# An encoder block on one Trainium2 core: the per-engine order of instructions chosen with the build tool's timeline model

## The chip, the core and the metric

The kernel runs on one NeuronCore of one Trainium2 chip. The metric is the device time of one execution in microseconds, and the time quoted is the median over runs. Engines are TensorE (PE in the profile, PEld its weight loads), VectorE (DVE), ScalarE (ACT), GpSimd (POOL) and SyncE (SP, which here only issues DMAs).

## What is computed

One encoder block over x of 512 rows and 2048 columns, all float32:

```
h   = rmsnorm(x) @ w_in                      # q, k, v, gates of both branches
a   = diff_attention(rope(q), rope(k), v)    # 8 heads, 2 softmaxes each
m   = mlstm(q', k', v', gates), both directions  # 4 heads
mix = sigmoid(branch gates) * projections of the normed a and m
x1  = x + mix @ w_out
y   = x1 + (silu(g) * u) @ w_ffn_out ;  g, u = rmsnorm(x1) @ w_ffn_in   # 5632 wide
out = rmsnorm(y)
```

In attention each head has two score matrices. Each is put through a softmax over its 512 keys, and the head uses `p = p0 - lam * p1`, then `p @ v`, then a norm over the head's 128 columns.

## The kernel before

Every float32 product is made of three products of parts: `split` (L148 to L150) copies a tile to a rounded high part on ScalarE and subtracts it on VectorE to get the low part, and `mm3` (L143 to L146) multiplies high by high, high by low and low by high. Large products use a scheme of seven block products in place of eight, so VectorE also adds weight blocks (L348 to L362) before they are split. Weights come through SP in pieces of 512 KB (`load`, L192 to L198, six raw buffers); a piece is cast to `whi_...` and subtracted to `wlo_...` (three buffers each) two pieces ahead of its use.

In time the program goes through these stages: projections for values and gates (to about 505 us), attention with the q and k projections of the next heads beside it (to 870), mLSTM (to 1000), branch projections (to 1160), the output projection wo (to 1360), the first FFN product `fi` in eleven column blocks (to 2230), and the second FFN product `fo` in two halves (to the end).

The order of the work is set in two steps. First the Python program issues instructions in an order written by hand. The projections are generators (`chunks`), and `advance(ns)` (in `build`) runs them for as many nanoseconds of TensorE work as it is given; a function handed to `later(ns, fn)` is issued when that much work has been issued since. In attention, `attn(h)` goes through four query tiles of 128 rows:

```python
        scores(0)
        advance(FILL)
        turn(0)
        scores(1)
        advance(FILL)
        turn(1)
        scores(2)
        values(0)
```

`scores(qt)` issues four products into two PSUM tiles `s{h}_{qt}_0` and `_1` (L1050, L1051), for each a maximum on VectorE (`nm`, L1052) and an exponential on ScalarE (`e`, L1054), then a reciprocal, two scalings and a sum on VectorE (L1058 to L1061). `turn(qt)` transposes that sum on TensorE into `tp{h}_{qt}` (L1071) and splits it into `pTh` and `pTl`, and `values` multiplies those by the values into `ha{h}`. `FILL` is 5600, so 5.6 us of projection products (`aqk...`, `mqk...`, `mv...`) are issued between the scores and the transposes. After the last value product of a head come a copy and a square of `ha`, its row sums on TensorE (`hss{h}`, L1108 and L1109), GpSimd's power (L544, `hrs`), and a product with a diagonal (`hbc{h}`, L551 and L552) that spreads the result over columns.

Second, the Tile framework's scheduler takes the issued instructions with their dependencies and chooses the final order on each engine by a cost model of its own; semaphores are then placed for that order. Each engine executes its list in order. Which cost model it uses is a switch of the context that `kernel` opens (L1476).

## Time and profile before

| | us |
|---|---|
| median of 3 runs | 2681.12 |
| lowest and highest | 2680.89, 2682.58 |
| profiled execution | 2683.64 |
| its span | 2681.9 |
| TensorE busy in it | 2605.4 |

The page gives busy time by engine, the span in 40 slices with the granted TensorE clock, the chain of work that ended last, and groups of instructions. An answer about waits names the engine and its operation, then what released it. A row of a timeline has a start, a duration, the engine, the line, and written tile <- read tiles; brackets hold the idle time before it.

### The profile page before, as it was taken

What the parts mean: (1) busy time and instruction counts of PE and PEld (TensorE: products, weight loads), DVE (VectorE), ACT (ScalarE), POOL (GpSimd) and SP (SyncE); (2) the same over time, 40 slices, a digit from 0 to 9 for tenths busy, and PEclk for the clock granted to TensorE, in tenths of its full rate; (3) what the DMA queues carried; (4) which work ended last, traced back from release to release, by engine and by line L of the source; (5) the groups of instructions that cost most, each with busy time, mean ns of one, the idle gap of its engine ahead of it and who ended that gap; (6) DMA issues with size and microseconds to landing.
All of it is one profiled execution on the core that took longest, in us unless ns stands there. A gap on an engine that the chain in (4) does not pass through costs nothing.

```text
span 2681.9 us, 33178 instructions
## 1 busy us (share of the span) xinstructions
PE 2605.4 (97%) x12136; PEld 2160.3 (81%) x12136; DVE 2129.2 (79%) x2692; ACT 1312.8 (49%) x1848; POOL 254.9 (10%) x448
## 2 busy tenths in 40 slices
PE   8999999999999999999899999999999999999997
PEld 7888888877878998887778888888888878777876
DVE  8977788777877676596788888888888889888885
ACT  8544444444544463345464444444444446546654
POOL 1000000011110113101110000000000002222211
PEclk9999999989999999999999999999999999999999
DMA  7655666633432346437665555555555578777763
GB/s 263 233 186 185 201 200 216 223 103 116 123 110 71 115 134 241 175 130 233 223 199 183 194 165 181 195 192 186 175 199 173 181 284 286 252 249 257 242 220 94
DMA packets 162227, 508.97 MB, mean 190 GB/s; under 512 B 21832, under 2 KB 22120, under 8 KB 162064
## 3 DMA queue, kind: packets, MB, share of 16 engines
q1 hardware_dynamic: 111456, 379.77, 41.3%
q0 software_dynamic: 33712, 97.71, 12.1%
q10 hardware_dynamic: 16896, 29.37, 3.1%
q8 instruction: 95, 1.56, 0.2%
q14 instruction: 68, 0.56, 0.1%
HBM read 445.41 MB, written 50.87 MB: 185 GB/s over the span
## 4 chain that ended last, share of the span: by engine, by line
PE 71%; DVE 12%; issue 7%; DMA 7%; ACT 2%; POOL 1%; SPq 0%; DVEq 0%; POOLq 0%; ACTq 0%
PE fi_b L145 12%; PE fi_c L145 8%; PE fi_a L145 8%; PE fo_b L145 4%; PE aqk_b L145 3%; PE fo_c L145 3%; PE fo_a L145 3%; PE mqk_b L145 3%; PE mv_p L145 3%; PE ba_p L145 3%; PE bm_p L145 3%; PE ga_b L145 2%; PE gm_b L145 2%; PE gm_a L145 1%; PE gm_c L145 1%
## 5 line engine op out<-in xcount | busy, mean ns | idle before, releaser
L145 PE MATMUL aqk_b<-xs,whi_aqk 128*128 128x512 f32 x512 | 162.0, 396 | 0.0
L149 ACT CAST whi_fi_Q<-fi_Q_t 128x1024 fp32r<-128x1024 f32 x88 | 92.5, 1052 | 117.7 <-PE fi_b L145 97.7
L145 PE MATMUL fi_a<-whi_fi_Q,h_X 128*128 128x512 f32 x440 | 147.0, 391 | 0.0
L145 PE MATMUL fi_c<-whi_fi_Q,h_S 128*128 128x512 f32 x440 | 145.0, 390 | 0.0
L145 PE MATMUL fi_b<-whi_fi_Q,h_S 128*128 128x512 f32 x352 | 115.5, 389 | 0.0
L145 PEld LDWEIGHTS aqk_b<-xs,whi_aqk 128*128 128x128 f32 x512 | 97.1, 191 | 19.6
L150 DVE TENSOR_TENSOR wlo_fi_Q<-fi_Q_t,whi_fi_Q 128x1024 fp32r<-128x1024 f32 x88 | 106.5, 1220 | 5.5 <-ACT whi_fi_Q L149 5.3
L145 PE MATMUL aqk_b<-xs,wlo_aqk 128*128 128x512 f32 x256 | 100.8, 394 | 0.0
L145 PEld LDWEIGHTS fi_c<-whi_fi_Q,h_S 128*128 128x128 f32 x440 | 83.0, 189 | 17.3
L145 PEld LDWEIGHTS fi_a<-whi_fi_Q,h_X 128*128 128x128 f32 x440 | 82.6, 188 | 16.8
L362 DVE TENSOR_TENSOR raw_fi_e<-raw_fi_e,raw_fi_f 128x1024 f32<-128x1024 f32 x44 | 53.9, 1224 | 52.6 <-DMA raw_fi_e<-in_w_ffi 52.6
L988 POOL DMA_DIRECT2D fs_X<-fg_X11d x22 | 11.9, 539 | 830.5 <-DVE wlo_fi_Q L150 785.3
L145 PE MATMUL fi_a<-wlo_fi_Q,h_X 128*128 128x512 f32 x220 | 85.9, 390 | 0.6 <-DVE wlo_fi_Q L150 0.6
L145 PE MATMUL fi_c<-wlo_fi_Q,h_S 128*128 128x512 f32 x220 | 85.8, 390 | 0.0
L348 DVE TENSOR_TENSOR raw_fi_b<-raw_fi_b,raw_fi_a 128x1024 f32<-128x1024 f32 x44 | 53.8, 1224 | 36.0 <-DMA raw_fi_b<-in_w_ffi 33.6
L149 ACT CAST whi_fi_Q<-raw_fi_e 128x1024 fp32r<-128x1024 f32 x44 | 46.4, 1055 | 72.6 <-PE fi_b L145 51.4
L145 PE MATMUL ba_p<-whi_ba,hahl 128*128 128x512 f32 x256 | 81.8, 390 | 0.0
L145 PE MATMUL mqk_b<-xs,whi_mqk 128*128 128x512 f32 x256 | 80.9, 396 | 0.0
L145 PE MATMUL bm_p<-whi_bm,hmhl 128*128 128x512 f32 x256 | 80.5, 391 | 0.0
L149 ACT CAST whi_fi_Q<-raw_fi_b 128x1024 fp32r<-128x1024 f32 x44 | 46.5, 1057 | 68.8 <-PE fi_c L145 52.1
L149 ACT CAST whi_fi_Q<-raw_fi_f 128x1024 fp32r<-128x1024 f32 x44 | 46.5, 1056 | 68.3 <-PE fi_c L145 63.9
L145 PEld LDWEIGHTS fi_b<-whi_fi_Q,h_S 128*128 128x128 f32 x352 | 66.1, 188 | 13.7
(843 smaller groups left out, 8479.5 us busy)
## 6 DMA issues: line engine op xcount, KB each, us to landing
raw_fi_a<-in_w_ffi SPq DMA_DIRECT2D x44, 512.0 KB, 3.4
raw_fi_b<-in_w_ffi SPq DMA_DIRECT2D x44, 512.0 KB, 4.2
raw_fi_c<-in_w_ffi SPq DMA_DIRECT2D x44, 512.0 KB, 4.1
raw_fi_d<-in_w_ffi SPq DMA_DIRECT2D x44, 512.0 KB, 4.2
raw_fi_f<-in_w_ffi SPq DMA_DIRECT2D x44, 512.0 KB, 3.5
raw_fi_e<-in_w_ffi SPq DMA_DIRECT2D x44, 512.0 KB, 3.6
raw_aqk<-in_w_aqk SPq DMA_DIRECT2D x32, 512.0 KB, 3.5
raw_fo_a<-in_w_ffo SPq DMA_DIRECT2D x20, 512.0 KB, 4.5
```

The source lines that it names most:

```text
L145: T.matmul(dst, lhs[l], rhs[r], start=first and i == 0, stop=last and i == 2, skip_group_check=skip)
L149: A.copy(hi, src)
L150: V.tensor_tensor(lo, src, hi.bitcast(F32), ALU.subtract)
L348: V.tensor_tensor(raws[r12], raws[r12], raws[r11], ALU.add)
L362: V.tensor_tensor(raws[r12], raws[r12], raws[r22], ALU.add)
L988: G.dma_start(got[n], fgd[g][f_].rearrange("p (k c) -> p k c", k=2))
```

## The change

The context is opened with a switch: the scheduler orders instructions by a timeline model in place of its default one. The program's own order of issue, its buffers and its arithmetic stay as they are.

```diff
-    with tile.TileContext(nc) as tc:
+    with tile.TileContext(nc, schedule_with_timeline_sim=True) as tc:
```

Of 11,527 rows that stand for TensorE's list, 9,219 lines of difference arise; VectorE's list of 2,690 rows has 3,143 and SP's of 776 has 294. Three places on TensorE follow. In the rows a product is `written<-stationary,moving` with its shape, `x2` is two such in a row, and the last number of a name is only the scheduler's.

TensorE in head 0 around the second query tile, before (`s` are scores, `tp` the transposes, `aqk2` a projection of q and k for later heads):

```order
L1051 MATMUL s0_1_0_4940<-k0_l0_4722,q0_h0_4708 128x512
L1050 MATMUL s0_1_1_4946<-k0_h1_4721,q0_h1_4709 128x512
L1051 MATMUL s0_1_1_4946<-k0_l1_4723,q0_h1_4709 128x512
L145 MATMUL aqk2_b0_4782<-xs14_4360,wlo_aqk2_30_4817 128x512
L145 MATMUL aqk2_b1_4783<-xs14_4360,whi_aqk2_30_4816 128x512 x2
L145 MATMUL aqk2_b1_4783<-xs14_4360,wlo_aqk2_30_4817 128x512
L145 MATMUL aqk2_b0_4782<-xs15_4363,whi_aqk2_30_4816 128x512 x2
L145 MATMUL aqk2_b0_4782<-xs15_4363,wlo_aqk2_30_4817 128x512
L145 MATMUL aqk2_b1_4783<-xs15_4363,whi_aqk2_30_4816 128x512 x2
L145 MATMUL aqk2_b1_4783<-xs15_4363,wlo_aqk2_30_4817 128x512
L1071 MATMUL tp0_1_4993<-ident_78,e0_1_0_4944 128x128 x4
L1050 MATMUL s0_2_0_5002<-k0_h0_4720,q0_h0_4708 128x512
```

and after:

```order
L145 MATMUL aqk2_b0_4782<-xs15_4363,wlo_aqk2_30_4817 128x512
L145 MATMUL aqk2_b1_4783<-xs15_4363,whi_aqk2_30_4816 128x512
L1051 MATMUL s0_0_1_4861<-k0_l1_4723,q0_h1_4709 128x512
L145 MATMUL aqk2_b1_4783<-xs15_4363,whi_aqk2_30_4816 128x512
L145 MATMUL aqk2_b1_4783<-xs15_4363,wlo_aqk2_30_4817 128x512
L1071 MATMUL tp0_0_4931<-ident_78,e0_0_0_4859 128x128 x4
L1050 MATMUL s0_1_0_4940<-k0_h0_4720,q0_h0_4708 128x512
L1051 MATMUL s0_1_0_4940<-k0_l0_4722,q0_h0_4708 128x512
L1050 MATMUL s0_1_1_4946<-k0_h1_4721,q0_h1_4709 128x512
L1051 MATMUL s0_1_1_4946<-k0_l1_4723,q0_h1_4709 128x512
L1071 MATMUL tp0_1_4993<-ident_78,e0_1_0_4944 128x128 x4
L1050 MATMUL s0_2_0_5002<-k0_h0_4720,q0_h0_4708 128x512
```

The ten `aqk2` products that stood between the last score product and `tp0_1` are gone from there, most of them to a place ahead of these scores; the transposes stand right behind.

TensorE in head 3 at its fourth query tile, before (rows 5 to 16 of the piece, more `aqk6` products, are left out):

```order
L1050 MATMUL s3_3_1_6185<-k3_h1_5493,q3_h1_5481 128x512
L1051 MATMUL s3_3_1_6185<-k3_l1_5495,q3_h1_5481 128x512
L145 MATMUL aqk6_b1_5976<-xs11_4281,whi_aqk6_20_5979 128x512
L145 MATMUL aqk6_b1_5976<-xs11_4281,wlo_aqk6_20_5980 128x512
...
L145 MATMUL aqk6_b0_5975<-xs15_4363,whi_aqk6_30_6047 128x512 x2
L145 MATMUL aqk6_b0_5975<-xs15_4363,wlo_aqk6_30_6048 128x512
L1071 MATMUL tp3_3_6232<-ident_78,e3_3_0_6183 128x128 x4
L1050 MATMUL s4_0_0_6276<-k4_h0_5802,q4_h0_5790 128x512
```

and after, from the third tile's transposes on:

```order
L1071 MATMUL tp3_2_6170<-ident_78,e3_2_0_6086 128x128 x4
L1050 MATMUL s3_3_0_6179<-k3_h0_5492,q3_h0_5480 128x512
L1051 MATMUL s3_3_0_6179<-k3_l0_5494,q3_h0_5480 128x512
L1050 MATMUL s3_3_1_6185<-k3_h1_5493,q3_h1_5481 128x512
L1051 MATMUL s3_3_1_6185<-k3_l1_5495,q3_h1_5481 128x512
L1071 MATMUL tp3_3_6232<-ident_78,e3_3_0_6183 128x128 x4
L1050 MATMUL s4_0_0_6276<-k4_h0_5802,q4_h0_5790 128x512
L1051 MATMUL s4_0_0_6276<-k4_l0_5804,q4_h0_5790 128x512
L1050 MATMUL s4_0_1_6282<-k4_h1_5803,q4_h1_5791 128x512
L1051 MATMUL s4_0_1_6282<-k4_l1_5805,q4_h1_5791 128x512
```

The 23 `aqk6` products that stood between `s3_3` and `tp3_3` are gone from there, and the transposes stand right behind the scores.

TensorE at the norm of head 0, beside the first tiles of head 1, before:

```order
L145 MATMUL ha0_4852<-pTl0_2_5078,av0_h1_4845 128x256
L145 MATMUL ha0_4852<-pTh0_2_5077,av0_l1_4847 128x256
L145 MATMUL aqk3_b0_5057<-xs9_4229,whi_aqk3_20_5061 128x512 x2
L145 MATMUL aqk3_b0_5057<-xs9_4229,wlo_aqk3_20_5062 128x512
L145 MATMUL aqk3_b1_5058<-xs9_4229,whi_aqk3_20_5061 128x512 x2
L145 MATMUL aqk3_b1_5058<-xs9_4229,wlo_aqk3_20_5062 128x512
...
L1108 MATMUL hss0_5257<-hsh0_5191,ones_r_85 128x512
L145 MATMUL aqk3_b0_5057<-xs12_4302,whi_aqk3_30_5119 128x512
L145 MATMUL aqk3_b0_5057<-xs12_4302,wlo_aqk3_30_5120 128x512
L1109 MATMUL hss0_5257<-hsl0_5192,ones_r_85 128x512
```

and after:

```order
L145 MATMUL ha0_4852<-pTl0_2_5078,av0_h1_4845 128x256
L145 MATMUL ha0_4852<-pTh0_2_5077,av0_l1_4847 128x256
L1108 MATMUL hss0_5257<-hsh0_5191,ones_r_85 128x512
L1109 MATMUL hss0_5257<-hsl0_5192,ones_r_85 128x512
L1071 MATMUL tp1_0_5269<-ident_78,e1_0_0_5208 128x128 x4
L1050 MATMUL s1_1_0_5278<-k1_h0_4899,q1_h0_4887 128x512
L1051 MATMUL s1_1_0_5278<-k1_l0_4901,q1_h0_4887 128x512
L1050 MATMUL s1_1_1_5284<-k1_h1_4900,q1_h1_4888 128x512
L1051 MATMUL s1_1_1_5284<-k1_l1_4902,q1_h1_4888 128x512
L552 MATMUL hbc0_5326<-hbc0_d0_5327,ones_83 128x128
```

The row sums `hss0` stand right behind the last value product `ha0`, and `hbc0` behind one tile's transposes and scores.

## Rows read from the trace of the kernel before

**Rows 1.** The page, busy time per engine, and the granted clock in 40 slices.

```profile
PE 2605.4 (97%) x12136; PEld 2160.3 (81%) x12136; DVE 2129.2 (79%) x2692; ACT 1312.8 (49%) x1848; POOL 254.9 (10%) x448
...
PEclk9999999989999999999999999999999999999999
```

**Rows 2.** The page, shares of the chain that ended last, by engine.

```profile
PE 71%; DVE 12%; issue 7%; DMA 7%; ACT 2%; POOL 1%; SPq 0%; DVEq 0%; POOLq 0%; ACTq 0%
```

**Rows 3.** Windows by stage; columns as in their first row.

```profile
core 0: us, PE busy (x) PEld busy (x) DVE busy (x) ACT busy (x) POOL busy (x), PEclk, DMA share, GB/s
...
100.00:505.00 405.00, 402.96 (x1771) 331.52 (x1771) 329.62 (x345) 197.86 (x219) 7.71 (x14) 1.00 0.62 208
505.00:870.00 365.00, 345.88 (x1748) 288.24 (x1747) 272.14 (x473) 161.05 (x290) 44.72 (x76) 0.97 0.36 109
...
1160.00:1360.00 200.00, 188.69 (x835) 152.04 (x834) 149.89 (x163) 102.25 (x156) 26.31 (x40) 0.97 0.64 207
1360.00:2230.00 870.00, 864.70 (x3886) 714.84 (x3885) 730.65 (x761) 403.18 (x452) 12.74 (x22) 1.00 0.57 193
2230.00:2430.00 200.00, 193.64 (x842) 155.89 (x840) 171.06 (x191) 113.92 (x159) 43.61 (x77) 1.00 0.77 262
```

**Rows 4.** Waits of PE: total us, times, longest us.

```profile
PE tp L1071 <- DVE e L1061: 16.2, 10, 4.9
...
PE wo_a L145 <- DVE wlo_wo_Q L150: 6.6, 3, 3.2
...
PE s L1050 <- DMA k_h<-k_h: 1.8, 1, 1.8
```

**Rows 5.** Timeline, head 4, fourth query tile; start us, us, engine, line.

```profile
752.57 0.40 PE L1051 MATMUL s<-k_l,q_h 128*128 128x512 f32 x1
...
753.78 1.28 DVE L1052 TENSOR_REDUCE nm<-s 128x1 f32<-128x512 f32 x2
...
755.17 0.68 ACT L1054 ACTIVATE e<-s,nm 128x512 f32<-128x512 f32 x1
...
755.97 0.17 DVE L1058 RECIPROCAL rl<-lsum 128x2 f32<-128x2 f32 x1 [0.92 <-ACT e L1054]
...
756.42 0.48 DVE L1060 TENSOR_SCALAR e<-e,rl 128x512 f32<-128x512 f32 x1
...
756.95 0.75 DVE L1061 SCALAR_TENSOR_TENSOR e<-e,rl,e 128x512 f32<-128x512 f32 x1
...
757.84 1.09 PE L1071 MATMUL tp<-ident,e 128*128 128x128 f32 x4 [4.87 <-DVE e L1061]
```

**Rows 6.** Timeline, head 0, third query tile: last score product and sum.

```profile
588.49 0.63 PE L1051 MATMUL s<-k_l,q_h 128*128 128x512 f32 x1
...
591.84 0.75 DVE L1061 SCALAR_TENSOR_TENSOR e<-e,rl,e 128x512 f32<-128x512 f32 x1
```

**Rows 7.** Timeline, head 0, the norm chain beside head 1.

```profile
611.53 0.69 DVE L1102 TENSOR_TENSOR hsq<-hr 128x512 f32<-128x512 f32 x1
...
612.91 0.69 DVE L150 TENSOR_TENSOR hsl<-hsq,hsh 128x512 fp32r<-128x512 f32 x1 [0.69 <-ACT hsh L149]
...
613.75 0.41 PE L1109 MATMUL hss<-hsl,ones_r 128*128 128x512 f32 x1
...
616.72 1.26 POOL L544 TENSOR_TENSOR hrs<-pw_in,mhalf 128x4 f32<-128x4 f32 x1 [1.53 <-DVE pw_in L543]
...
618.01 0.29 DVE L551 TENSOR_SCALAR hbc_d<-ident,hrs 128x128 f32<-128x128 f32 x1 [0.94 <-POOL hrs L544]
```

**Rows 8.** Windows of the eight stretches at the lower clock between 500 and 2660 us.

```profile
756.10:762.90 6.80, 5.06 (x18) 4.51 (x19) 3.47 (x7) 1.46 (x3) 0.00 (x0) 0.50 0.36 102
...
sum 40.80, PE 36.26 PEld 29.75 DVE 26.55 ACT 16.12 POOL 3.53; mean PE 4.53 PEld 3.72 DVE 3.32 ACT 2.01 POOL 0.44
```

**Rows 9.** The chain, FFN stretch: start us, us, what.

```profile
1418.28 5.44 PE fi_b L145 x24
```

**Rows 10.** The page, ACT casts of FFN weights: busy, mean ns, idle before.

```profile
L149 ACT CAST whi_fi_Q<-fi_Q_t 128x1024 fp32r<-128x1024 f32 x88 | 92.5, 1052 | 117.7 <-PE fi_b L145 97.7
```

## The prediction, written before the changed kernel was timed

> **What bounds the kernel now.** I read the page first. TensorE is busy 97% of the span, VectorE 79%, ScalarE 49% [rows 1], and the chain that ended last is TensorE's for 71% [rows 2]. So the time is TensorE's work plus the waits that interrupt it, and nothing else counts unless it makes TensorE wait. The work itself cannot shrink by reordering: 24 products of 512 columns stand end to end in 5.44 us, 0.227 us each [rows 9], and both orders hold the same products. Of the span of 2681.9 us (the profiled execution took 2683.6) TensorE is idle for 76.5 [rows 1], start and end among it. That, with what a lower clock costs (below), is all an order can win; an order can lose any amount.
>
> Next the windows by stage, to see where those microseconds sit. The FFN's first half is idle for 5.3 us in 870; attention (505 to 870 us) for 19.1 in 365; the output projection (1160 to 1360) for 11.3 in 200 [rows 3]. The waits of TensorE name the largest single cause: the attention transposes `tp` wait 16.2 us for the softmax sum `e`, ten times, at most 4.9 us; wo's products wait 6.6 us for a split weight [rows 4].
>
> The timeline at one such wait shows the price of a missing cover. For head 4, fourth query tile, no other product stands between the last score product (start 752.57) and the transposes (757.84). In between come VectorE's two maxima, ScalarE's exponentials, the reciprocal, the scaling and the sum [rows 5]. The gap is 5.27 us less the product's own 0.23: **5.0 us**. The same chain ran in 4.1 us where it was quickest: product at 588.49, sum done at 592.59 [rows 6], or 3.9 less the product. In rows 5 nothing else was queued on the chain; where VectorE has a weight to subtract between the steps it is longer. TensorE must have about 5 us of other products there, or it stands. In the order before, 29 of 32 query tiles have over 4 us, mostly 5 to 10.
>
> **The change, part by part.** It adds and removes no arithmetic; it moves instructions on all engines. What matters is what stands between producer and consumer on TensorE, which the order listing shows and the rows price.
>
> *Softmax cover.* I counted, for each of the 32 (head, tile) pairs, the other products between the last score product and the transposes, at 0.227 us per 512 columns [rows 9] and in proportion for narrower ones. After the change eleven pairs have 3.3 us or less, where before there were three: (0,0) 0.45, (0,1) 0, (1,1) 0.87, (2,0) 3.24, (3,2) 1.43, (3,3) 0, (4,2) 2.30, (4,3) 0, (5,2) 1.43, (6,1) 0.45, (7,1) 0.67. The products that covered them have gone to other pairs, which now have up to 17.5 us where 5 would do, and there they cover nothing. Eleven chains of 5.0 us less these covers leave 44.2 us. The row of before says 16.2 us [rows 4], so the term is **+28**. Bounds: at 3.9 us per chain, 32 us are left, +16; and since the same counting gives only 12.1 us for the waits of before that measured 16.2, a third more is possible: 59, or +43. I take 28, since rows 5 is the case that recurs: bare, with no cover.
>
> *Norm chain of each head.* After the last value product of a head come a copy, a square and a split, then the row sum `hss`; after it a masked product, a reduction, GpSimd's power and the diagonal, then `hbc` [rows 7]. From square (611.53) to split done (613.60) is 2.07 us, to which the copy's 0.6 and a handover are to be added: about 2.9. From `hss` (613.75) to the diagonal done (618.30) is 4.5, less its own 0.2 product: about 4.1. Before, 4.3 us or more of other products stand in each place and TensorE does not wait. Now the cover is 0 for `hss` of heads 0 and 7 and 1.3 for head 1; for `hbc` it is 1.3 for heads 0 and 5 and 0 for head 6. That is 2.9 + 2.9 + 1.6 + 2.8 + 2.8 + 4.1 = 17 us. The `hbc` waits of heads 0 and 6 lie inside the same stretch as the short tiles (1,1) and (7,1), whose sum then has time to finish, so 5 are not counted twice: **+12**; bounds 6 and 17.
>
> *Clock.* After a long stop the granted clock fell to 0.50, that is to 1.2 GHz. Between 500 and 2660 us there are eight such stretches, 40.8 us long, in which TensorE was busy 36.3 [rows 8]; half of that busy time, 18 us, is what they cost, 2.3 us for each. All eight follow stops of TensorE of 1.9 to 5 us. By the covers above, stops of that size rise from four in attention to about eleven places that are not next to each other: 7 x 2.3 = **+16**. Bounds: 7 (three stretches) and 30 (every added stop has a stretch of 6.8 us [rows 8]).
> The Trainium skill (TensorE: Matmul & The Clock Gate, section "What's actually happening") holds the ramp to be under 1% of a typical kernel's span and not worth modelling; by that the sum would be 16 us lower. The rows agree that it is under 1% now, 18 of 2682 us, but it is paid once per stop, and this change adds stops.
>
> *Start of blocks.* The first product of six projection blocks (av0 three times, ga1, gm0, gm1) now stands right behind the cast of its weight rather than some products later; a cast takes 1.05 us [rows 10], so **+6**; bounds 0 and 10. *First scores.* Their 1.8 us wait for a key load [rows 4] gets more cover: **-2**.
>
> *Costed at nothing.* In the FFN's first half VectorE's sums for later weights stand seven to nine places earlier and some subtractions later. There ScalarE waits for TensorE to release a buffer (117.7 us of idle before its casts [rows 10]), so casts run as far ahead as buffers allow; cast and subtraction together take 2.3 us and the piece is needed one group of 24 products, 5.4 us, later [rows 9]. The 3 us of slack cover one extra VectorE operation of 1.2 us, not three. In wo and the FFN's second half pieces shift both ways; I take 0, with 15 us either way, the wait of one row above twice [rows 4].
>
> Sum: 28 + 12 + 16 + 6 - 2 = +60 on the profiled 2683.6 gives 2743.6. The median of the runs, 2681.1, lies 2.5 below that execution, so I forecast **2741**.
>
> **Rivals.**
> *Faster, by a model that is right elsewhere.* The timeline order may feed TensorE better where the present order leaves it idle: wo's 11.3 us, the 6.4 of the second FFN half's first 200 us [rows 3], the start. Of the 76.5 us of idle time, attention's 19.1 and the first FFN half's 5.3 leave 52; with start and end never quite gone, 45 are to be had. It decides if more than the attention's loss is recovered, whose floor by the bounds is 16 + 6 + 7 = 29. Both together: 2681 - 45 + 29 = 2665. For it speaks that wo waits for split weights, which an order can advance; against it that wo and FFN weights come from the same in-order engines and a DMA share of 0.77 [rows 3], and that I see pieces moved later as often as earlier. 0.07.
>
> *No change.* Losses at the floor, 29, against gains of the same size: 2681, 0.05. That the option does nothing is excluded: most of TensorE's rows stand elsewhere.
>
> *Slower by much more, through loads.* On SP's queue ten loads of x, 256 KB each, now go ahead of the last weights of the gate projection (about 470 to 485 us). At that stage's 208 GB/s [rows 3] 2.6 MB are 12.6 us, and a weight that is late by it stops TensorE. If likewise one FFN slack of 3 us is overrun by one subtraction per block, eleven blocks give 11 x 1.2 = 13, and wo with the second half their 15: 2741 + 13 + 13 + 15 = 2782. Against it: loads are issued several pieces ahead. 0.15.
>
> *As forecast*, attention's terms within their bounds: 0.73.
>
> **How the numbers follow.** The low bounds give 2681 + 16 + 6 + 7 - 2 = 2708, and with 10 won in wo 2698; the high ones run with the load rival to 2785. The range 2698 to 2785 leaves out the first two rivals and a little on top, under 2 in 10. A measurement of this kernel can tell 0.2%, 5.4 us, from no change: faster 0.07, same 0.05, slower 0.88.
>
> **What would show it.** In the profile after: the row of `tp` waiting for `e` rises from 16 to 40 to 60 us in ten or more stops; new rows of `hss` and `hbc` waiting; eight or more further stretches at 0.50 between 570 and 880 us; attention's window 50 us longer; FFN's first half within 5 us of its 870. I am wrong if `tp` waits under 25 us in all, if the added time sits after 1000 us, or if TensorE's idle time in wo falls by over 10 us.

## The result, and the profile after

The changed kernel takes 2822.61 us (median of 4 runs, 2821.15 to 2824.71) against 2681.01 before (the median of the three runs of before and a fourth): **ratio 1.0532, 95% interval 1.0514 to 1.0550**, slower by 141.6 us. The direction was forecast, the size was not: the range ended at 2785. The profiled execution has a span of 2822.9 us.

The page after, busy time and granted clock, as [rows 1] of before:

```profile
PE 2649.9 (94%) x12136; PEld 2171.9 (77%) x12136; DVE 2124.5 (75%) x2692; ACT 1307.7 (46%) x1848; POOL 254.2 (9%) x448
...
PEclk9999999989989999999999999999999999999999
```

TensorE has the same 12,136 instructions and is idle for 173.0 us in place of 76.5; it is also busy for 44 us longer, part of it at the lower clock (one more slice of the row below nine tenths). VectorE and ScalarE are busy as long as before, to within some 5 us. So no work was added; TensorE waits.

The windows by stage, with the stages' new bounds (columns: stretch, width, busy time by engine, granted clock, share of the DMA engines, GB/s), as [rows 3]:

```profile
core 0: us, PE busy (x) PEld busy (x) DVE busy (x) ACT busy (x) POOL busy (x), PEclk, DMA share, GB/s
0.00:505.00 505.00, 465.11 (x2052) 377.39 (x2053) 382.01 (x444) 249.25 (x341) 22.12 (x48) 0.99 0.59 197
541.00:930.00 389.00, 337.08 (x1645) 282.29 (x1644) 255.23 (x434) 150.29 (x268) 43.27 (x74) 0.91 0.32 98
930.00:1060.00 130.00, 120.75 (x774) 110.38 (x773) 72.51 (x167) 51.76 (x107) 15.14 (x25) 0.96 0.31 100
...
1287.00:1460.00 173.00, 166.05 (x747) 133.99 (x746) 136.88 (x149) 92.58 (x143) 25.71 (x40) 0.99 0.71 225
1460.00:2330.00 870.00, 847.51 (x3733) 683.08 (x3733) 696.30 (x722) 384.52 (x430) 8.42 (x14) 1.00 0.55 183
```

The first row lies in the projections, which now last to 541 us. The others are attention up to its last head (its last transposes start at 966, where before they started at 869), the rest of it with mLSTM, wo with its transposes, and 870 us of the first FFN product. In the last of them TensorE is idle for 22.5 us where before it was 5.3; in the 505 us of the first it is idle for 40 us, where before it was some 15.

To price the stages whatever their length I sorted TensorE's instructions by the tile that they write, and added up by how much the distance from one start to the next exceeds what that width takes at full clock (0.2265 us for 512 columns, and the median of each narrower width). The sums, the excess of each stage, in us:

| stage | before | after | difference | forecast |
|---|---|---|---|---|
| first value projection | 13.1 | 9.0 | -4.1 | 0 |
| value and gate projections | 4.9 | 44.3 | +39.4 | +6 |
| attention | 37.2 | 93.0 | +55.8 | +54 |
| mLSTM, branch projections | 3.6 | 22.4 | +18.8 | 0 |
| wo and its transposes | 24.5 | 13.8 | -10.7 | 0 |
| first FFN product | 6.9 | 46.2 | +39.3 | 0 |
| second FFN product | 21.2 | 23.9 | +2.7 | 0 |
| sum | 111.3 | 252.5 | +141.2 | +60 |

The sum accounts for the measured 141.6. Attention came out as forecast in its sum; the two stages of streamed weights, at 39 us each, did not. One trace stands on each side, and small differences are not all the change's: in the twelve traces of this case whose order of wo is the one before, wo has 15.7 to 24.7 us, so that the 24.5 of this table is near the top.

TensorE's waits after (total us, times, longest), as [rows 4]:

```profile
PE tp L1071 <- DVE e L1061: 46.2, 13, 8.4
PE fi_b L145 <- DVE wlo_fi_Q L150: 16.7, 30, 2.4
...
PE hbc L552 <- DVE hbc_d L551: 7.4, 3, 7.0
PE mtp L1277 <- DVE mh L1270: 6.7, 1, 6.7
...
PE hss L1108 <- ACT hsh L149: 4.3, 2, 2.2
...
PE wo_a L145 <- DVE wlo_wo_Q L150: 2.2, 1, 2.2
```

The transposes `tp` went from 16.2 to 46.2 us, the norm's `hss` and `hbc` appear with 4.3 and 7.4, and `wo_a` fell from 6.6 to 2.2. Not forecast are the FFN's `fi_b` (30 small waits, 0.5 us in two before) and mLSTM's `mtp`. At head 3's fourth query tile, whose 23 products of cover are gone, the timeline shows the same bare chain as [rows 5]:

```profile
776.52 0.63 PE L1051 MATMUL s<-k_l,q_h 128*128 128x512 f32 x1
...
776.81 0.69 DVE L150 TENSOR_TENSOR pTl<-tp,pTh 128x512 fp32r<-128x512 f32 x1
777.42 1.28 DVE L1052 TENSOR_REDUCE nm<-s 128x1 f32<-128x512 f32 x2
...
780.58 0.75 DVE L1061 SCALAR_TENSOR_TENSOR e<-e,rl,e 128x512 f32<-128x512 f32 x1
...
781.48 1.09 PE L1071 MATMUL tp<-ident,e 128*128 128x128 f32 x4 [4.33 <-DVE e L1061]
```

From the last score product (776.52) to the transposes (781.48) are 4.96 us, 0.3 us less than in [rows 5]. At the two other tiles without any cover, head 0's second and head 4's fourth, it is 4.25 and 4.57 us. The three waits are 4.3, 3.6 and 4.2 us.

Some waits are of another kind. At head 0's first tile two products stand between scores and transposes, and TensorE waits 8.40 us:

```profile
610.64 0.39 PE L1051 MATMUL s<-k_l,q_h 128*128 128x512 f32 x1
...
612.17 1.22 DVE L150 TENSOR_TENSOR wlo_aqk<-raw_aqk,whi_aqk 128x1024 fp32r<-128x1024 f32 x1
...
617.17 0.67 DVE L603 SCALAR_TENSOR_TENSOR q_l<-q_t,q_h 64x512 fp32r<-64x512 f32 x1
...
618.99 0.75 DVE L1061 SCALAR_TENSOR_TENSOR e<-e,rl,e 128x512 f32<-128x512 f32 x1
...
619.88 1.09 PE L1071 MATMUL tp<-ident,e 128*128 128x128 f32 x4 [8.40 <-DVE e L1061]
```

Between the steps of this chain VectorE does other work: it subtracts weights and prepares q and k of later heads. Head 4's second tile waits in the same way, 4.9 us, though 11.4 us pass there after the last score product. At the first tiles of heads 1 and 2 (2.8 and 6.2 us) the exponentials, whose maxima were done some 5 us before, stand on ScalarE behind the norm's copy and cast of the head before, which wait for that head's last value products. These four waits make 22.3 of the 46.2 us. Their chains are not new: at the first tiles of heads 0, 1 and 2 they took 11.1, 13.2 and 10.6 us in the kernel before, but there other products covered them, and TensorE waited 0, 0.7 and 0.6 us.

### The profile page after: what moved, and what is told of

The parts are those of the page before. It is cut to its first block, busy times and chain, and to the rows that moved or that the text cites. A ratio compares the mean times of both kernels' runs of the same rounds, so it can differ in the third digit from the quotient of the medians.

```text
span 2822.9 us, 33273 instructions
## 1 busy us (share of the span) xinstructions
PE 2649.9 (94%) x12136; PEld 2171.9 (77%) x12136; DVE 2124.5 (75%) x2692; ACT 1307.7 (46%) x1848; POOL 254.2 (9%) x448
## 3 DMA queue, kind: packets, MB, share of 16 engines
q8 instruction: 95, 1.56, 0.2%
## 5 line engine op out<-in xcount | busy, mean ns | idle before, releaser
L149 ACT CAST whi_fi_Q<-raw_fi_a 128x1024 fp32r<-128x1024 f32 x44 | 46.1, 1048 | 63.3 <-PE fi_a L145 36.6
```

Source lines behind the costliest of these rows:

```text
L149: A.copy(hi, src)
```

## The experiments

All kernels below are the kernel before with the order of some instructions imposed. The instructions have the same names in both builds, so an order can be written down and imposed: after the program is issued, one order-only dependency is added between each instruction and the next on its engine. The dependency itself brings no wait, and buffers and operations stay. No run imposes the order before with nothing moved; but the first FFN product, where its order is left as it was in all five lists, has 5.6 to 8.6 us of excess in the six runs that impose all five lists with another stage moved, against 6.9 before.

```diff
             build(ctx, tc, a, out)
+            order_edges(nc, tc, ORDERS)
...
+    for engine, text in orders.items():
...
+        for x, y in zip(order, order[1:]):
+            tc.add_manual_dep(mine[y], mine[x].name, only, reason="order")
```

### One stage at a time

`ORDERS` is the order before on all five engines, and the instructions of one stage (a range of the program's instruction numbers) are laid into the same places in the changed order.

```diff
+ORDERS = {engine: before, with 0 to 4350 as after}        # s_proj
+ORDERS = {engine: before, with 4350 to 10800 as after}    # s_attn
+ORDERS = {engine: before, with 12200 to 18850 as after}   # s_ffn1
+ORDERS = {engine: before, with 10800 to 12200 and from 18850 as after}   # s_wofo
```

**s_proj.** 

> The order of the changed kernel on all five engines for the instructions up to the end of the value and gate projections, the order before for everything else. Theory (each stage pays for its own order, by waits inside it): the trace after has 35 us more idle or slow TensorE time between 0 and the end of these projections than the trace before, so 2681 + 35 = 2716, within 8. Rival (the stages are coupled: the late weights and the shifted loads of one stage are what the next pays for): a stage alone costs under half of what stands in its window, so below 2700. My prediction had costed this stage at 6 us: 2687.

**s_attn.** 

> The changed order for the instructions of attention, mLSTM and the branch projections alone. Theory (local waits): the trace after has 55 us more in attention and 19 more in mLSTM and branch projections: 2681 + 74 = 2755, within 10. Rival (coupled stages): below 2720. My prediction had 54 for attention and nothing for what follows: 2735.

**s_ffn1.** 

> The changed order for the instructions of the first FFN product alone. Theory (local waits): 39 us more in that window, so 2681 + 39 = 2720, within 8. Rival (coupled): below 2700. My prediction had 0 here: 2681.

**s_wofo.** 

> The changed order for the instructions of the output projection wo and of the second FFN product fo alone. Theory (local waits): wo and the transposes behind it have 11 us less, fo 3 us more: 2681 - 8 = 2673, within 6, a small gain. Rival (coupled: wo only gained because attention before it was slower and its weights had more time): 2681 or slower.

Measured, against 2676.54 on the same chip (the ratios, here and below, are worked out from all runs and can differ a little from those of the medians):

| run | us | ratio, 95% interval |
|---|---|---|
| s_proj | 2715.55 | 1.0138, 1.0117 to 1.0160 |
| s_attn | 2755.46 | 1.0291, 1.0275 to 1.0308 |
| s_ffn1 | 2718.20 | 1.0156, 1.0139 to 1.0173 |
| s_wofo | 2682.43 | 1.0018, 1.0007 to 1.0030 |

The first three are what the trace's stage accounts said: 37, 78 and 42 us (1.38%, 2.91% and 1.56% of 2677) for 35, 75 and 39. By the same count over their traces attention alone has 92.8 us of excess (93.0 in the whole change), the first FFN product 45.8 (46.2). So the three stages pay for their own order; coupling between stages, the rival, is out as the main cause. The fourth was a miss: wo fell to 14.5 us as expected, but the second FFN product rose by ten to 31.9, where the same order costs 23.9 in the whole change. Why was not tried. The four together make 6.0%, more than the 5.3% of the whole.

### One engine at a time

```diff
+ORDERS = {all but TensorE: before, with 12200 to 18850 as after; TensorE: before}   # m_fi_notpe
+ORDERS = {TensorE: before, with 12200 to 18850 as after; the others: before}        # m_fi_pe
+ORDERS = {TensorE: after}     # b_PEa, default model for the other engines
+ORDERS = {TensorE: before}    # a_PEb, timeline model for the other engines
```

**m_fi_notpe.** 

> First FFN product: the changed order on VectorE, ScalarE, GpSimd and SP, TensorE keeps the order before; everything else as before. Theory V (VectorE's order makes the loss: the next block's sums now stand ahead of the subtractions of the pieces Q41 and Q42, which TensorE works off in 2.7 us each): most of the 41 us that this stage cost alone, 2700 to 2720. Rival P (TensorE's order makes it: the transposes that stood between those pieces are gone, so its own cover is missing): under 10 us, 2680 to 2688.

**m_fi_pe.** 

> First FFN product: the changed order on TensorE alone, the other engines and everything else as before. Theory V: under 12 us, 2677 to 2689. Rival P: 30 to 41 us, 2707 to 2718. If both runs of the pair come out well under 41 us, it takes both moves at once.

**b_PEa.** 

> TensorE's list in the changed order in the whole kernel; the lists of the other engines are chosen for it by the default model. Theory (in attention TensorE's own list makes the loss, in the FFN VectorE's): attention keeps its 55 us and the stages behind it some 15, the FFN costs under 12, the projections about half of their 37: 2681 + 90 = 2770, between 2750 and 2790. Rival (VectorE's list makes the attention loss too, as chains are split by other operations): under 2725.

**a_PEb.** 

> The mirror: TensorE's list as before in the whole kernel, the other engines' lists chosen for it by the timeline model. Theory: attention's loss is gone but for 10 us, the FFN's stays at 25 to 40, the projections' at about half: 2681 + 55 = 2736, between 2715 and 2755. Rival: attention's loss stays, 2770 or more.

Measured, against 2684.47:

| run | us | ratio, 95% interval |
|---|---|---|
| m_fi_notpe | 2748.51 | 1.0240, 1.0225 to 1.0255 |
| m_fi_pe | 2702.52 | 1.0060, 1.0045 to 1.0075 |
| b_PEa | 2813.58 | 1.0483, 1.0466 to 1.0501 |
| a_PEb | 2812.25 | 1.0475, 1.0458 to 1.0492 |

None of the four landed where I put it. In the FFN the other engines' lists alone cost 64 us and TensorE's alone 16, while both together cost 42: TensorE's new list partly fits the new lists of the others. With TensorE's old list its transposes of the gated product `fg_T` wait for VectorE's result, a wait that neither the kernel before nor the changed one has among TensorE's:

```profile
PE fg_T L849 <- DVE fu L929: 16.9, 20, 1.5
```

The whole-kernel pair has a clearer side. With TensorE's changed list, and the other lists chosen for it by the default model, attention's excess is 95.1 us, as much as in the whole change:

```profile
PE tp L1071 <- DVE e L1061: 45.2, 11, 6.6
```

With TensorE's old list, and the other lists chosen for it by the timeline model, it is 46.8, and the wait of `tp` is nearly back to its 16.2, while `fg_T` waits again:

```profile
PE fg_T L849 <- DVE fu L929: 21.4, 22, 2.6
PE tp L1071 <- DVE e L1061: 17.7, 10, 4.7
```

So attention's loss follows TensorE's list, whichever model chose the others, as a missing cover would. The first tiles with their long chains wait in b_PEa too, 6.0 us at head 0 and 6.3 at head 2. That the totals of both runs are still near 1.048 comes from elsewhere. By the same count a_PEb has 90.6 us in the first FFN product and 35.7 in the projections, b_PEa 33.0 and 18.6; the cause of these was not taken apart.

### The price of missing cover

```diff
-    FILL = 5600
+    FILL = 2800
```

**fill2800.** 

> The kernel before, default model, with FILL 2800 in place of 5600: half the cover in attention, nothing else changed. By the order listing the covers fall so that 32 chains of 5.0 us less their cover leave 73 us, where before 12 was left and 16 measured. Theory (a chain costs 5.0 us less its cover, and each added stop of over 1.9 us, 13 more, costs 2.3 by the lower clock): tp waits 65 to 85 us in all, the time 2682 + 61 + 30 = 2773, between 2750 and 2795. Rival (with less between them VectorE and ScalarE finish a chain sooner, 3.9 us): tp waits near 51, time 2682 + 35 + 25 = 2742 or less.

Measured: 2760.49 against 2683.63, ratio 1.0288 (1.0261 to 1.0316). The time lies in the theory's range, but TensorE's wait for the sum is the rival's:

```profile
PE tp L1071 <- DVE e L1061: 53.7, 17, 5.0
PE s L1050 <- DMA k_h<-k_h: 9.6, 5, 2.9
```

The first row is what 3.9 us a chain gives (51), not 5.0 (73). The second was in neither account: the score products now wait for loads of keys, 9.6 us where before it was 1.8. So the time came out near the theory partly by luck. In the changed kernel too a bare chain costs less than 5.0: 3.6 to 4.3 us of wait at its three tiles without cover. Its 46.2 us are near the 44.2 worked out at 5.0 only because of the four long chains told of with the result. The softmax cover alone, with nothing else moved, was not tried.

### What moves in the FFN

```diff
+ORDERS = {VectorE: before, ten times fi_Q60_t2 and fi_Q61_t2 ahead of wlo_fi_Q41 and wlo_fi_Q42; others: before}   # f_sums
+ORDERS = {as s_ffn1, and VectorE: these twenty sums behind wlo_fi_Q43}   # f_back
```

**f_sums.** 

> The kernel before with one edit on VectorE: in ten FFN column blocks the next block's two sums (L356, for Q60 and Q61) are moved up, ahead of the subtractions for Q41 and Q42, where the changed order has them. Theory (these two sums make the recurring waits at Q41 and Q42, 0.6 and 0.75 us in the trace after): the row of fi_b waiting for wlo_fi_Q appears with ten to twenty times, and the time rises by 6 to 14 us, 2688 to 2696 against a before of 2682. Rival (TensorE's transposes, which the order before keeps between Q41 and Q42, cover them, so both moves are needed): within 3 us of before.

**f_back.** 

> The kernel with the changed order in the first FFN product alone (41 us slower than before), with the same twenty sums put back behind the subtraction for Q43. Theory: the waits at Q41 and Q42 go, 14 us, so 2682 + 27 = 2709, within 6. Rival (the place of single sums does not matter, the subtractions are late because the whole list of VectorE runs late): 2718 or more.

f_sums measured 2690.47 against 2683.63, ratio 1.0020 (1.0002 to 1.0039), at the low edge of what was expected. Its first FFN product has 13.3 us of excess, 6.4 more than before, and the wait is there, though eight times in place of ten to twenty:

```profile
PE fi_b L145 <- DVE wlo_fi_Q L150: 3.6, 8, 0.9
```

f_back was to win 14 us of s_ffn1's loss and doubled it: 2772.20, ratio 1.0320 (1.0287 to 1.0354). That fells the theory that a sum costs its own 1.2 us of VectorE time. VectorE's waits in its FFN stretch tell why:

```profile
DVE raw_fi_b L348 <- DMA raw_fi_b<-in_w_ffi: 107.2, 33, 5.3
...
DVE raw_fi_e L362 <- DMA raw_fi_e<-in_w_ffi: 89.3, 38, 4.8
```

VectorE stands for 107 us at the sums of `raw_fi_b`, waiting for loads, where before it stood for 31. The sums and subtractions also release the raw buffers (six of them) that the next loads need, as SP's waits before its loads show in this run:

```profile
SPq L197 <- DVE wlo_fi_Q L150: 580.8, 219, 8.1
SPq L197 <- DVE fi_Q_t L356: 177.5, 42, 15.0
```

So my reading is that a sum moved back makes the next load late, VectorE then waits for it at the next sum, and the subtractions queued behind that sum wait as well. The new theory, W, is that the whole pattern of sums against subtractions makes the loss. Two timelines fit it. Before, at the second weight piece of the block `fi6` (SP issues a load; the sum; the subtraction for Q40):

```profile
1811.40 0.33 SPq L197 DMA_DIRECT2D raw_fi_b<-in_w_ffi  x1
...
1815.62 1.23 DVE L348 TENSOR_TENSOR raw_fi_b<-raw_fi_b,raw_fi_a 128x1024 f32<-128x1024 f32 x1 [0.33 <-DMA raw_fi_b<-in_w_ffi]
...
1816.76 1.22 DVE L150 TENSOR_TENSOR wlo_fi_Q<-fi_Q_t,whi_fi_Q 128x1024 fp32r<-128x1024 f32 x1
```

and after, at the same piece, with the cast that the subtraction needs and TensorE's load of its result:

```profile
1932.44 0.33 SPq L197 DMA_DIRECT2D raw_fi_b<-in_w_ffi  x1
...
1934.02 1.05 ACT L149 CAST whi_fi_Q<-fi_Q_t 128x1024 fp32r<-128x1024 f32 x1 [1.68 <-PE fi_b L145]
...
1937.29 1.23 DVE L348 TENSOR_TENSOR raw_fi_b<-raw_fi_b,raw_fi_a 128x1024 f32<-128x1024 f32 x1 [3.09 <-DMA raw_fi_b<-in_w_ffi]
...
1939.03 1.22 DVE L150 TENSOR_TENSOR wlo_fi_Q<-fi_Q_t,whi_fi_Q 128x1024 fp32r<-128x1024 f32 x1
...
1940.30 0.19 PEld L145 LDWEIGHTS fi_b<-wlo_fi_Q,h_X 128*128 128x128 f32 x1 [0.85 <-DVE wlo_fi_Q L150]
```

Before, the load was issued 4.2 us ahead of the sum and VectorE waited 0.33 us. After, VectorE stands 3.09 us at the sum. The cast for Q40 has ended at 1935.07, so its subtraction could run, but stands behind the sum and ends at 1940.25; the weight load that needs it has been idle for 0.85 us, and TensorE's products for 0.42.

### The place of all sums

```diff
+ORDERS = {VectorE: before, its 175 FFN sums ahead of the same subtraction as after; others: before}   # g_A
+ORDERS = {as s_ffn1, and VectorE: these sums ahead of the same subtraction as before}   # g_B
+ORDERS = {VectorE: before, the 96 sums of 0 to 4350 ahead of the same subtraction as after; others: before}   # h_A
+ORDERS = {as s_proj, and VectorE: these sums ahead of the same subtraction as before}   # h_B
```

**g_A.** 

> The kernel before; on VectorE, in the first FFN product, all 175 sums of raw weights (L348, L356, L362, L369) stand ahead of the same subtraction as in the changed order. Nothing else is moved. Theory W (a sum that waits for its load holds up the subtractions queued behind it): most of the loss, 2682 + 30 to 60. Rival E (the sums' place matters little; the loss comes from evacuations, transposes and TensorE's list): under 12 us.

**g_B.** 

> The changed order in the first FFN product (41 us slower than before when it stands alone), with the same 175 sums put back ahead of the same subtraction as in the order before. Theory W: the loss falls below 15 us, 2682 to 2697. Rival E: it stays at 30 to 45, 2712 to 2727. Third possibility (the lists fit each other, and any mixture is worse than either): above 2727.

**h_A.** 

> The same as g_A in the value and gate projections: the kernel before with only the 96 sums of raw weights of that stage on VectorE placed as in the changed order. Theory W: 20 to 39 us slower, 2702 to 2721. Rival E: under 10 us.

**h_B.** 

> The same as g_B in the value and gate projections: the changed order of that stage (37 us slower alone) with the 96 sums put back. Theory W: under 15 us slower, 2682 to 2697. Rival E: 25 to 37 us slower, 2707 to 2720. Third possibility (a mixture is worse than either): above 2722.

Measured, against 2678.53:

| run | us | ratio, 95% interval |
|---|---|---|
| g_A | 2732.06 | 1.0200, 1.0180 to 1.0220 |
| g_B | 2689.46 | 1.0039, 1.0023 to 1.0054 |
| h_A | 2700.46 | 1.0077, 1.0057 to 1.0096 |
| h_B | 2695.57 | 1.0058, 1.0043 to 1.0074 |

In the FFN theory W holds in both directions: moving the sums brings the loss, and putting them back takes most of it away. The place of the sums alone costs 54 us in the order before; put back, it takes s_ffn1's 42 down to 10. VectorE's waits for loads in that stage follow. Before:

```profile
DVE raw_fi_e L362 <- DMA raw_fi_e<-in_w_ffi: 52.6, 33, 3.5
...
DVE raw_fi_b L348 <- DMA raw_fi_b<-in_w_ffi: 31.3, 20, 4.6
DVE fi_Q_t L369 <- DMA raw_fi_d<-in_w_ffi: 5.5, 4, 2.5
```

after the whole change:

```profile
DVE raw_fi_e L362 <- DMA raw_fi_e<-in_w_ffi: 84.9, 39, 5.1
DVE raw_fi_b L348 <- DMA raw_fi_b<-in_w_ffi: 52.0, 21, 3.3
DVE fi_Q_t L356 <- DMA raw_fi_c<-in_w_ffi: 14.7, 18, 2.2
DVE fi_Q_t L369 <- DMA raw_fi_d<-in_w_ffi: 8.9, 18, 0.9
```

in g_A, with only the sums moved:

```profile
DVE raw_fi_e L362 <- DMA raw_fi_e<-in_w_ffi: 99.2, 38, 4.3
DVE raw_fi_b L348 <- DMA raw_fi_b<-in_w_ffi: 58.7, 36, 3.7
...
DVE fi_Q_t L356 <- DMA raw_fi_c<-in_w_ffi: 3.1, 2, 1.5
...
DVE fi_Q_t L369 <- DMA raw_fi_d<-in_w_ffi: 1.6, 3, 1.1
```

and in g_B, with only the sums put back:

```profile
DVE raw_fi_e L362 <- DMA raw_fi_e<-in_w_ffi: 32.2, 29, 2.6
DVE raw_fi_b L348 <- DMA raw_fi_b<-in_w_ffi: 28.5, 17, 3.3
...
DVE fi_Q_t L369 <- DMA raw_fi_d<-in_w_ffi: 6.7, 11, 3.5
DVE fi_Q_t L356 <- DMA raw_fi_c<-in_w_ffi: 4.3, 3, 2.4
```

These rows add up to 89 us before, 161 after, 163 in g_A and 72 in g_B. In the projections the sums are half of it: 21 us when moved alone, and with them back 16 of 37 remain. In h_B TensorE's longest wait there, after those of the start, is for a cast (`av_c` for `whi_av_Q`, 4.7 us in two); which move makes this other half was not tried.

### A version that keeps the gains

```diff
+ORDERS = {engine: before, with 0 to 700 and 10800 to 12200 as after}   # best
```

**best.** 

> The order before in the whole kernel but for two stages where the trace after shows less idle time: the first value projection (4 us less) and the output projection wo with the transposes behind it (11 us less). If the gain is those stages' own: 2682 - 14 = 2668, between 2664 and 2674. Rival (in the run with wo and fo changed wo fell by 10 us but fo rose by 10: what wo gains is handed on as a later wait): 2680 to 2684.

Measured: 2674.91 against 2683.63 (12 and 23 runs), ratio 0.9967, interval 0.9953 to 0.9982. It is faster than the kernel before by 0.33%, some 9 us of the 14 expected, and so than the changed one. By the count above the first value projection has 10.2 us (13.1 before), wo 13.2 (24.5), and TensorE's wait in wo is

```profile
PE wo_a L145 <- DVE wlo_wo_Q L150: 2.4, 2, 1.7
```

in place of 6.6. The second FFN product has 25.2 us for 21.2, which may look as if part of the gain were handed on, as the rival said. It is not shown: with its order unchanged that stage has 20.2 to 27.1 us in the traces of this case, and wo 15.7 to 24.7. Against such values of wo, 11 us was too much to expect.

## Why the prediction was wrong

**Bound: right. Price of a wait: a little high.** TensorE's work did not change, and every microsecond lost is a wait or a lower clock. The three bare chains took 4.2 to 5.0 us from product to transposes, or 4.0 to 4.7 less the product, for the 5.0 of the sum.

**Softmax cover: the mechanism right, the size partly luck.** Forecast +28; the row of `tp` rose by 30.0 (16.2 to 46.2). b_PEa and a_PEb show that it follows TensorE's list: 45.2 and 17.7. But of the eleven pairs in the sum, nine waited 23.6 us in all, not 37.9: bare chains are cheaper than 5.0, and (7,1) did not wait at all. The first tiles of heads 0 and 2 waited 14.6 for 6.3, and three pairs that the sum did not have waited 8.0. The step that was off is the one price for every chain: a first tile's chain took 10.6 to 13.2 us before the change too, where the sum had 5.0, and ScalarE's part in it was not foreseen. The two errors nearly cancel.

**Norm chain: right in its sum.** Forecast +12; `hss` and `hbc` wait 4.3 and 7.4 us, where before `hbc` waited 0.9. `hss` waits at heads 0 and 7, as forecast, though not at head 1. Of `hbc` one wait makes 7.0, at head 6, for 4.1; at heads 0 and 5, 2.8 each in the sum, it is 0.2 and none.

**Clock: right in attention.** Stretches at 0.50 rose there from four to ten, where seven more were forecast. Of attention's excess I counted what products in stretches at 0.50 took beyond their own pace: 9.2 us before, 22.4 after, so +13 for +16. In the whole kernel it is 17.8 and 39.4, since other stages added stops.
The rule of the Trainium skill that I set against it (TensorE: Matmul & The Clock Gate, section "What's actually happening": under 1% of a typical kernel's span) is not met by the changed kernel: 39 us are 1.4% of 2823, and the 22 added are 15% of the loss.

**Costed at nothing: here it failed.** I wrote of the FFN that "the 3 us of slack cover one extra VectorE operation of 1.2 us, not three", with a group of 24 products, 5.4 us, per piece, and left the term at 0. Two things were wrong in that step. The row of 24 products [rows 9] is two pieces: the stage has 308 casts for 3,696 products, so a piece serves 12, 2.7 us, against 2.3 us of cast and subtraction. By that reckoning the slack is 0.4 us, not 3. And I priced a moved sum as VectorE time. It is a wait: a sum stands at the head of VectorE's list until its load lands, and holds up ready subtractions. [rows 10] told me that casts run ahead; the row that mattered, VectorE's wait for loads (89 us of standing in this stage before), is not among my rows, because TensorE hardly felt it: its excess there was 6.9. The order before had placed these waits where they did little harm. What the runs put in place of the 0 is 39 us in this stage (42 in s_ffn1), of which 32 go when the sums alone are put back (g_B).

**Start of blocks: in part the same failure.** Forecast +6 for six casts; measured +39, of which the sums are about 21 (h_A). The cause of the rest is open.

**mLSTM: left out.** I looked for short covers in attention only. Behind it TensorE waits as well, `mtp` 6.7 us once and `mn` 6.5 in three waits; the stage lost 19. That cover is missing there too was not tried.

**The range.** The rival that went furthest had its price from one subtraction per block and from x loads. The x loads did not show: from their issue (497 us) to the end of the projections TensorE has no wait over 0.7 us. It was right in its place (weights that come late in FFN and projections) and far too small. The end of the range, 2785, is also no sum of the terms: the high bounds together give 2779.

**wo: a gain.** I took 0 with 15 either way; the trace gave -10.7, part of which is the spread of wo from trace to trace.

## What to carry to other kernels

Before you call a move on an in-order engine free, list what that engine waits for, not only what the bound engine waits for: an operation that waits for a transfer is a gate for all that stands behind it, and its place in the list is worth its wait, not its duration. Before you take slack from a group in a view, count how many pieces the group holds. When a sum comes out right, check its terms one by one: two errors can cancel. Lists of one plan can depend on each other: mixing one engine's list with another's from a different plan cost more than either plan here (m_fi_notpe), while putting one kind of operation back (g_B) won most of a stage's loss. So measure a plan by stages, keep the stages that gain, and time the mixture.

## What was not expected

Moving twenty sums later by four to seven places on VectorE cost another 44 us (1.56% to 3.20%), though VectorE had nothing more to do; it stood longer at the sums for their loads. And taking a stage's order for all engines kept the stages' losses nearly additive, while taking it for one engine did not: 64 and 16 us apart, 42 together.
